# Six single loads become three pair loads of 64 KB pieces, and gamma arrives in four transfers

## The chip, the cores and the metric

The kernel runs on one core of a Trainium2 chip. The metric is the device time of one execution in microseconds (us), lower is better. The kernel before takes about 317.0 us, and equal kernels differ by a few tenths from run to run, so this study is about effects near 0.1%: most of its work went into telling such an effect from noise and into finding where it sits.

## The reference

```python
rms = np.sqrt(np.mean(x ** 2, axis=-1, keepdims=True) + eps)
out = gamma * x / rms
return 0.5 * out * (1 + np.tanh(np.sqrt(2 / np.pi) * (out + 0.044715 * out ** 3)))
```

x has 8 x 1024 rows of 2048 numbers in float32. So 67.1 MB are read and 67.1 MB are written, with an RMS norm over each row and a GELU between.

## The kernel before

The 8192 rows are cut into 16 groups of 512 (4 rows for each of 128 partitions, 4 MB a group). Six buffers ("slots", in three pairs that lie side by side) hold groups in flight. SyncE issues the loads, ScalarE issues the stores. A load waits until the store of the group six places earlier has landed, as it uses the same slot.

```python
def pair_part(a, k):          # two groups: 8 rows = 64 KB in a row for each partition
    n = 2 * R * P
    return a[k * n : (k + 1) * n].rearrange("(p r) d -> p r d", p=P)

def part(a, g):               # one group; 32 KB in a row for each partition
    if g // 2 in (LOAD_PAIR, STORE_PAIR):
        return pair_part(a, g // 2)[:, g % 2 * R : g % 2 * R + R, :]
    return a[g * R * P : (g + 1) * R * P].rearrange("(p r) d -> p r d", p=P)

def load(g):
    nc.sync.dma_start(out=slot[g % SLOTS], in_=part(x2, g))
...
for g in range(G + 1):
    if g < G:
        squares(g, ...)            # ScalarE, the other rows on VectorE
        ...
        inverse_rms(g)             # VectorE and GpSimd
        scale(g, 0, R)             # VectorE: x * gamma
    if g:
        gelu(g - 1)                # ScalarE
        store(g - 1)               # issued by ScalarE
        if g - 1 + SLOTS < G:
            load(g - 1 + SLOTS)    # issued by SyncE
```

Only groups 2 and 3 are loaded as a pair, and only 12 and 13 are stored as one. Each engine works its own list in order, so ScalarE does not start GELU of group g-1 before the squares of group g, for which load g must have landed.

Of the kernel before, what the change touches and what calls it, by code (L numbers as in the profile page):

```python
# [7 lines left out]
FP32 = mybir.dt.float32  # L8
# [3 lines left out]
P = 128  # L12
ROWS = 4
SLOTS = 6

LOAD_PAIR = 1
STORE_PAIR = 6

GW = 128

NARROW = 128

# [1 line left out]
@with_exitstack  # L24
def kernel(
    ctx: ExitStack,
    tc: tile.TileContext,
    x: bass.AP,
    gamma: bass.AP,
    eps: bass.AP,  # L30
    out: bass.AP,
):





    nc = tc.nc
    D = x.shape[-1]
    R = ROWS  # L40
    eps_f = float(eps)
    x2 = x.rearrange("b s d -> (b s) d")
    o2 = out.rearrange("b s d -> (b s) d")
    G = x2.shape[0] // (P * R)

    def pair_part(a, k):

        n = 2 * R * P
        return a[k * n : (k + 1) * n].rearrange("(p r) d -> p r d", p=P)

    def part(a, g):

        if g // 2 in (LOAD_PAIR, STORE_PAIR):
            return pair_part(a, g // 2)[:, g % 2 * R : g % 2 * R + R, :]
        return a[g * R * P : (g + 1) * R * P].rearrange("(p r) d -> p r d", p=P)

    sbuf = ctx.enter_context(tc.tile_pool(name="sbuf", bufs=1))
    psum = ctx.enter_context(
        tc.tile_pool(name="psum", bufs=1, space=bass.MemoryType.PSUM)
    )  # L60
    pair = [
        sbuf.tile([P, 2 * R, D], FP32, name=f"pair{i}") for i in range(SLOTS // 2)
    ]
    slot = [pair[i // 2][:, i % 2 * R : i % 2 * R + R, :] for i in range(SLOTS)]
    spare = sbuf.tile([P, D // GW, GW + 16], FP32, name="spare")
    gamma_row = spare[0:1]
    ones = sbuf.tile([1, P], FP32, name="ones")
    warm = sbuf.tile([1, 1], FP32, name="warm")
    power = sbuf.tile([P, R], FP32, name="power")
    ssq = sbuf.tile([P, G, R], FP32, name="ssq")  # L70
    rstd = sbuf.tile([P, G, R], FP32, name="rstd")
    ms = sbuf.tile([P, R], FP32, name="ms")
    y = sbuf.tile([P, R], FP32, name="y")
    z = sbuf.tile([P, R], FP32, name="z")
    gamma_ps = psum.tile([P, D], FP32, name="gamma_ps")
    junk = psum.tile([P, D], FP32, name="junk")

    def on_vector(g):

        return 1 if g % 3 else 2  # L80

    def load(g):
        nc.sync.dma_start(out=slot[g % SLOTS], in_=part(x2, g))  # L83

    def squares(g, r, n):
        for q in range(r, r + n):
            nc.scalar.activation(  # L87
                out=junk,
                in_=slot[g % SLOTS][:, q, :],
                func=ACT.Square,  # L90
                accum_out=ssq[:, g, q : q + 1],
            )

    def squares_on_vector(g, r, n):
        for q in range(r, r + n):
            row = slot[g % SLOTS][:, q, :].rearrange("p (a b) -> p a b", b=GW)
            nc.vector.scalar_tensor_tensor(  # L97
                out=spare[:, :, 0:GW], in0=row, scalar=1.0, in1=row,
                op0=ALU.bypass, op1=ALU.mult, accum_out=ssq[:, g, q : q + 1],
            )  # L100

    def inverse_rms(g):

        v = nc.vector
        v.tensor_scalar(  # L105
            out=ms, in0=ssq[:, g, :], scalar1=1.0 / D,
            scalar2=eps_f, op0=ALU.mult, op1=ALU.add,
        )
        m_, y_, z_ = ms, y, z
        nc.gpsimd.tensor_tensor(  # L110
            out=y_, in0=m_, in1=power, op=ALU.pow
        )
        v.tensor_tensor(out=z_, in0=m_, in1=y_, op=ALU.mult)  # L113
        v.scalar_tensor_tensor(  # L114
            out=z_, in0=z_, scalar=-0.5, in1=y_, op0=ALU.mult, op1=ALU.mult
        )
        v.scalar_tensor_tensor(  # L117
            out=rstd[:, g, :], in0=z_, scalar=1.5, in1=y_,
            op0=ALU.add, op1=ALU.mult,
        )  # L120

    def scale(g, r, n):
        rows = slot[g % SLOTS][:, r : r + n, :]
        nc.vector.tensor_tensor(  # L124
            out=rows,
            in0=rows,
            in1=gamma_ps.unsqueeze(1).to_broadcast([P, n, D]),
            op=ALU.mult,
        )

    def gelu(g):
        for r in range(R):
            nc.scalar.activation(  # L133
                out=slot[g % SLOTS][:, r, :],
                in_=slot[g % SLOTS][:, r, :],
                func=ACT.Gelu_apprx_tanh,
                scale=rstd[:, g, r : r + 1],
            )

    def store(g):  # L140
        if g:
            if g // 2 != STORE_PAIR:
                nc.scalar.dma_start(out=part(o2, g), in_=slot[g % SLOTS])  # L143
            elif g % 2:
                nc.scalar.dma_start(
                    out=pair_part(o2, g // 2), in_=pair[g // 2 % (SLOTS // 2)]
                )
            return
        src = pair[0].rearrange("p r d -> p (r d)")
        dst = part(o2, 0).rearrange("p r d -> p (r d)")  # L150
        for a, z in ((0, NARROW), (NARROW, R * D)):
            nc.scalar.dma_start(out=dst[:, a:z], in_=src[:, a:z])

    with tc.manual_schedule():
        for g in range(SLOTS):
            if g // 2 != LOAD_PAIR:
                load(g)
            elif g % 2:
                nc.sync.dma_start(
                    out=pair[LOAD_PAIR], in_=pair_part(x2, LOAD_PAIR)  # L160
                )
        nc.scalar.dma_start(
            out=gamma_row[:, :, 0:GW],
            in_=gamma.rearrange("(o a b) -> o a b", o=1, b=GW),
        )
        nc.gpsimd.memset(power, -0.5)  # L166
        nc.vector.memset(warm, 0.0)  # L167
        nc.vector.memset(ones, 1.0)  # L168
        nc.scalar.activation(out=warm, in_=warm, func=ACT.Gelu_apprx_tanh)  # L169
        for k in range(0, D, 512):  # L170
            nc.tensor.matmul(  # L171
                out=gamma_ps[:, k : k + 512],
                lhsT=ones,
                rhs=gamma_row[:, k // GW : (k + 512) // GW, 0:GW],
                start=True,
                stop=True,
            )
        for g in range(G + 1):
            if g < G:
                squares(g, 0, R - on_vector(g))  # L180
                squares_on_vector(g, R - on_vector(g), on_vector(g))
                if g < G - 1:
                    inverse_rms(g)
                    scale(g, 0, R)
                else:
                    scale(g, 0, 1)
                    inverse_rms(g)
                    for r in range(1, R):
                        scale(g, r, 1)
            if g:  # L190
                gelu(g - 1)
                store(g - 1)
                if g - 1 + SLOTS < G:
                    load(g - 1 + SLOTS)
# [35 lines left out]
```

## Time and profile before

| | |
|---|---|
| time | 316.97 us, median of 3 runs; 317.01 with the 3 that were run beside the changed kernel |
| busiest compute engines | ScalarE 66%, VectorE 63% of the span |
| 16 transfer engines | 99% busy, 426 GB/s over the span |
| load queue waits for stores | 236.9 us, 11 times |

A profile like this is read from the transfer row first: no compute engine is near its limit, the transfer engines are. The lines themselves are in the prediction.

### The profile page before, as it was taken

The page shows a single profiled execution, that of the slowest core. Times are in us where ns is not written, and L with a number is a line of the kernel's source. Part 1 is how long each engine was busy: PE and PEld are TensorE (multiplying, and loading weights), DVE is VectorE, ACT ScalarE, POOL GpSimd, SP SyncE. Part 2 cuts the span into 40 slices and gives each one's busy share as a digit, 9 for nine tenths or more (in the row PEclk, how much of TensorE's full clock was granted, in tenths as well). Part 3 has the DMA queues.
Part 4 walks back from the last instruction along what each step waited for, and adds up shares of the span by engine and source line. Part 5 has one row for each costly group of instructions (what it writes and reads, how often), then busy time and mean ns, then how long its engine had stood idle before and what let it go on. Part 6 is the DMA issues. An engine that isn't in the chain of part 4 may idle for free.

```text
span 315.1 us, 457 instructions
## 1 busy us (share of the span) xinstructions
PE 7.2 (2%) x8; PEld 2.5 (1%) x8; DVE 198.5 (63%) x129; ACT 206.9 (66%) x150; POOL 16.4 (5%) x21
## 2 busy tenths in 40 slices
PE   0900000000000000000000000000000000000000
PEld 0300000000000000000000000000000000000000
DVE  0089887988989884639684393668727638781000
ACT  1327869999999749397590965929369295797000
POOL 0010101011010101010010100101001010010000
DMA  8999989999999999999999999999999999999896
GB/s 334 404 462 408 526 339 396 458 402 462 403 463 403 459 408 458 412 453 424 441 424 441 424 441 424 441 428 437 437 428 437 428 437 428 474 399 474 387 445 291
DMA packets 4498, 134.24 MB, mean 426 GB/s; under 512 B 512, under 2 KB 656, under 8 KB 656
## 3 DMA queue, kind: packets, MB, share of 16 engines
q1 hardware_dynamic: 2160, 67.11, 49.7%
q10 hardware_dynamic: 2336, 67.12, 49.3%
q14 instruction: 2, 0.02, 0.0%
HBM read 67.12 MB, written 67.11 MB: 426 GB/s over the span
## 4 chain that ended last, share of the span: by engine, by line
another core or an unknown queue 36%; DMA 36%; ACT 18%; issue 1%; SPq 1%; ACTq 0%
DMA pair<-in_x_dram 21%; DMA out_dram<-pair 15%; ACT pair L133 12%; ACT junk L87 6%; SPq L83 1%; ACTq L143 0%
## 5 line engine op out<-in xcount | busy, mean ns | idle before, releaser
L124 DVE TENSOR_TENSOR pair<-pair,gamma_ps 128x8192 f32<-128x8192 f32 (+1 forms) x19 | 139.2, 7334 | 0.0
L87 ACT ACTIVATE junk<-pair 128x2048 f32<-128x2048 f32 x42 | 79.0, 1881 | 78.7 <-DMA pair<-in_x_dram 76.2
L133 ACT ACTIVATE pair<-pair,rstd 128x2048 f32<-128x2048 f32 x64 | 122.6, 1987 | 2.3 <-DVE pair L124 1.9
L97 DVE SCALAR_TENSOR_TENSOR spare<-pair 128x2048 f32<-128x2048 f32 x22 | 50.4, 2291 | 39.3 <-DMA pair<-in_x_dram 24.6
L110 POOL TENSOR_TENSOR y<-ms,power 128x4 f32<-128x4 f32 x16 | 16.1, 1007 | 260.8 <-DVE ms L105 260.8
L105 DVE TENSOR_SCALAR ms<-ssq 128x4 f32<-128x4 f32 x16 | 2.7, 170 | 26.2 <-ACT junk L87 25.4
L113 DVE TENSOR_TENSOR z<-ms,y 128x4 f32<-128x4 f32 x16 | 2.6, 163 | 19.0 <-POOL y L110 19.0
L87 ACT ACTIVATION_READ_ACCUMULATOR junk<-pair 128x1 f32 x42 | 7.8, 186 | 0.0
L171 PE MATMUL gamma_ps<-spare,ones 1*128 1x512 f32 x8 | 7.2, 1072 | 8.3 <-DMA spare<-in_gamma_dram 8.3
L117 DVE SCALAR_TENSOR_TENSOR rstd<-z,y 128x4 f32<-128x4 f32 x16 | 2.6, 162 | 0.6
L114 DVE SCALAR_TENSOR_TENSOR z<-z,y 128x4 f32<-128x4 f32 x16 | 2.6, 162 | 0.6
L171 PEld LDWEIGHTS gamma_ps<-spare,ones 1*128 1x128 f32 x8 | 2.5, 326 | 11.4 <-issue 11.4
L169 ACT ACT_TABLE_LOAD x1 | 1.3, 1283 | 1.4 <-PEq L211 1.4
L97 DVE DVE_READ_ACCUMULATOR spare<-pair 128x1 f32 x22 | 1.8, 83 | 0.0
L167 DVE MEMSET warm<- 1x1 f32 x1 | 0.1, 59 | 0.8 <-PEq L211 0.8
L169 ACT ACTIVATE warm<-warm 1x1 f32<-1x1 f32 x1 | 0.2, 202 | 0.0
L168 DVE MEMSET ones<- 1x128 f32 x1 | 0.2, 165 | 0.0
L166 POOL MEMSET power<- 128x4 f32 x1 | 0.1, 101 | 0.3 <-POOLq L211 0.3
L211 POOL MEMSET const-float32-0.0<- 128x1 f32 x1 | 0.1, 98 | 0.2 <-issue 0.2
L211 POOL MEMSET const-bfloat16-1.0<- 128x1 bf16 x1 | 0.1, 102 | 0.0
L211 POOL MEMSET const-uint8-127<- 128x1 uint8 x1 | 0.1, 102 | 0.0
L211 POOL MEMSET const-float32-1.0<- 128x1 f32 x1 | 0.1, 98 | 0.0
## 6 DMA issues: line engine op xcount, KB each, us to landing
pair<-in_x_dram SPq DMA_DIRECT2D x14, 4096.0 KB, 25.5
out_dram<-pair ACTq DMA_DIRECT2D x13, 4096.0 KB, 52.4
out_dram<-pair ACTq DMA_DIRECT2D x1, 4032.0 KB, 31.3
out_dram<-pair ACTq DMA_DIRECT2D x1, 64.0 KB, 17.6
spare<-in_gamma_dram ACTq DMA_DIRECT2D x1, 8.0 KB, 7.4
pair<-in_x_dram SPq DMA_DIRECT2D x1, 40.5
out_dram<-pair ACTq DMA_DIRECT2D x1, 30.9
```

What stands on the lines that cost most here:

```text
L83: nc.sync.dma_start(out=slot[g % SLOTS], in_=part(x2, g))
L87: nc.scalar.activation(out=junk, in_=slot[g % SLOTS][:, q, :], func=ACT.Square, accum_out=ssq[:, g, q : q + 1],)
L97: nc.vector.scalar_tensor_tensor(out=spare[:, :, 0:GW], in0=row, scalar=1.0, in1=row, op0=ALU.bypass, op1=ALU.mult, accum_out=ssq[:, g, q ...
L105: v.tensor_scalar(out=ms, in0=ssq[:, g, :], scalar1=1.0 / D, scalar2=eps_f, op0=ALU.mult, op1=ALU.add,)
L110: nc.gpsimd.tensor_tensor(out=y_, in0=m_, in1=power, op=ALU.pow)
L113: v.tensor_tensor(out=z_, in0=m_, in1=y_, op=ALU.mult)
L114: v.scalar_tensor_tensor(out=z_, in0=z_, scalar=-0.5, in1=y_, op0=ALU.mult, op1=ALU.mult)
L117: v.scalar_tensor_tensor(out=rstd[:, g, :], in0=z_, scalar=1.5, in1=y_, op0=ALU.add, op1=ALU.mult,)
L124: nc.vector.tensor_tensor(out=rows, in0=rows, in1=gamma_ps.unsqueeze(1).to_broadcast([P, n, D]), op=ALU.mult,)
L133: nc.scalar.activation(out=slot[g % SLOTS][:, r, :], in_=slot[g % SLOTS][:, r, :], func=ACT.Gelu_apprx_tanh, scale=rstd[:, g, r : r + 1],)
L169: nc.scalar.activation(out=warm, in_=warm, func=ACT.Gelu_apprx_tanh)
L171: nc.tensor.matmul(out=gamma_ps[:, k : k + 512], lhsT=ones, rhs=gamma_row[:, k // GW : (k + 512) // GW, 0:GW], start=True, stop=True,)
```

## The change

The intent: fewer and larger pieces for a kernel that is bound by its transfers. Groups 6 to 11 are loaded in three pairs of 64 KB pieces, each issued when both of its buffers are free. Gamma is cut into four transfers, so that the kernel has 32 transfers in all as before. (Left out of the cut below: the padding of `spare`, which goes from 16 to 4 columns with the narrower rows, and the start, where the six loads are now all made by `load`.)

```diff
-LOAD_PAIR = 1
+LOAD_PAIRS = (1, 3, 4, 5)
-GW = 128
+GW = 32
+CHUNK = 512
...
-        if g // 2 in (LOAD_PAIR, STORE_PAIR):
+        if g // 2 in (*LOAD_PAIRS, STORE_PAIR):
...
     def load(g):
-        nc.sync.dma_start(out=slot[g % SLOTS], in_=part(x2, g))
+        if g // 2 not in LOAD_PAIRS:
+            nc.sync.dma_start(out=slot[g % SLOTS], in_=part(x2, g))
+        elif g % 2:
+            nc.sync.dma_start(
+                out=pair[g // 2 % (SLOTS // 2)], in_=pair_part(x2, g // 2)
+            )
...
-        nc.scalar.dma_start(
-            out=gamma_row[:, :, 0:GW],
-            in_=gamma.rearrange("(o a b) -> o a b", o=1, b=GW),
-        )
+        for k in range(0, D, CHUNK):
+            nc.scalar.dma_start(
+                out=gamma_row[:, k // GW : (k + CHUNK) // GW, 0:GW],
+                in_=gamma[k : k + CHUNK].rearrange("(o a b) -> o a b", o=1, b=GW),
+            )
```

More of the change, by code (lines that the diff above doesn't have):

```diff
@@ L64 @@
     slot = [pair[i // 2][:, i % 2 * R : i % 2 * R + R, :] for i in range(SLOTS)]
-    spare = sbuf.tile([P, D // GW, GW + 16], FP32, name="spare")
+    spare = sbuf.tile([P, D // GW, GW + 4], FP32, name="spare")
     gamma_row = spare[0:1]
@@ L155 @@
         for g in range(SLOTS):
-            if g // 2 != LOAD_PAIR:
-                load(g)
-            elif g % 2:
-                nc.sync.dma_start(
-                    out=pair[LOAD_PAIR], in_=pair_part(x2, LOAD_PAIR)
-                )
-        nc.scalar.dma_start(
-            out=gamma_row[:, :, 0:GW],
-            in_=gamma.rearrange("(o a b) -> o a b", o=1, b=GW),
-        )
+            load(g)
+        for k in range(0, D, CHUNK):
[3 more added lines that the diff above has]
+            )
         nc.gpsimd.memset(power, -0.5)
```

## The prediction

> **What bounds the kernel now.** I read the page from the top: busy shares, the slices, the queues, then the chain that ended last, the waits of the load queue, and the windows. The page first:
>
> ```profile
> span 315.1 us, 457 instructions
> PE 7.2 (2%) x8; PEld 2.5 (1%) x8; DVE 198.5 (63%) x129; ACT 206.9 (66%) x150; POOL 16.4 (5%) x21
> ...
> DMA  8999989999999999999999999999999999999896
> ...
> q1 hardware_dynamic: 2160, 67.11, 49.7%
> q10 hardware_dynamic: 2336, 67.12, 49.3%
> ```
>
> No compute engine is over 66% of the span, while the two queues (q1 has the loads, q10 the stores and gamma) together keep the 16 transfer engines busy 49.7 + 49.3 = 99.0% of it. That is the bound: 0.990 x 315.1 = 312 us of transfer work for each engine, and 3 us of idle at the two ends. The windows of the middle say the same, with a share of 1.00 and about 433 GB/s wherever one looks (last two columns: transfer share, GB/s):
>
> ```profile
> 60.00:120.00 60.00, 0.00 (x0) 0.00 (x0) 51.55 (x34) 51.71 (x39) 4.03 (x4) 1.00 1.01 436
> 120.00:240.00 120.00, 0.00 (x0) 0.00 (x0) 75.65 (x51) 81.32 (x60) 7.05 (x7) 1.00 1.00 433
> ```
>
> The chain shows what looks like a wait that could be removed:
>
> ```profile
> 147.25 0.33 SPq L83
> 147.58 18.99 another core or an unknown queue
> 166.67 0.04 issue
> 166.71 0.33 SPq L83
> 167.03 18.86 another core or an unknown queue
> ```
>
> and so do the waits of the load queue (total us, times, longest):
>
> ```profile
> SPq L83 <- DMA out_dram<-pair: 236.9, 11, 47.3
> ```
>
> Each load of groups 6 to 15 is issued when the store that frees its buffer has landed, one per 19.36 us (127.99 to 244.13 us in the chain is six periods). But one period moves one 4 MB load and one 4 MB store, 8.39 MB in 19.36 us, or 433 GB/s. So the wait of 236.9 us is a queue waiting behind a saturated resource, not the cause of the length. I also added up the single transfer records of the trace: the first data piece starts at 1.74 us, the last ends at 313.93, and the busy time of all pieces divided by 16 is 312.2 us, equal to that interval within 0.1. **There is no hole in the transfers to fill.** What can change the time is the work in them (number and cost of pieces), or a hole that the change opens.
>
> **What the Trainium skill says.** Its page "DMA: Bandwidth & Descriptors", section "Where 436 GB/s comes from", puts the ceiling of the 16 ports at 435 GB/s. The trace's 433 to 436 in the middle windows agrees. The same page, "Queues, rings and completion order", says that each engine takes turns between the queues that have work, a packet at a time. The trace agrees: the 512-byte pieces of the first narrow store start at 36.2, 38.6 and 41.1 us on one engine, one per 64 KB load piece of 2.42 us, and then every 1.23 us beside 32 KB load pieces. The same page, "Anatomy of one DMA", says that transfer engines do not wait on semaphores, the issuing sequencer does. That is how the page shows it: the wait stands in SPq. Its figure of about 2 us for set-up and completion fits too: the store of group 3 has its last piece end at 126.30, and the load that it frees is issued at 127.99, 1.7 us later. Last, "Specifications" warns of pieces under 512 bytes, which gamma's become.
>
> **The change part by part.** The listing of each engine's program shows the same order of instructions on all engines; SP issues 12 transfers for 15, ACT 20 for 17, 32 in all either way. The eight completion semaphores are handed round, so I went through the new waits that this makes.
>
> 1. Bigger pieces. The trace's transfer records give 1,213 ns for a 32 KB piece, 2,418 ns for a 64 KB piece (the pair load of groups 2 and 3 and the pair store of 12 and 13, both the same), 9 ns for a completion write. A pair of single loads costs an engine 16 x 1,213 + 2 x 9 = 19,426 ns; a pair load 8 x 2,418 + 9 = 19,353. Saved: 73 ns a pair, **0.22 us for three pairs**. As the engines are full throughout, all of it lies on the path that sets the end.
>
> 2. Gamma in four. One transfer of sixteen 512-byte pieces (27 ns each, one per engine) and a completion becomes four of sixteen 128-byte pieces. Per engine that is three more pieces and three more completions, at most 3 x (27 + 9) = 0.11 us (an estimate that charges 128 bytes as 512). ACT issues three more transfers at 0.60 us, 1.8 us, before 13.0 us, when it has its first data: hidden. But each small piece takes its turn behind a load piece of 1.21 us, and so does each completion. Before, gamma landed after 7.4 us; four transfers are eight turns, six more than now, so the last may land some 7 us later, about 15 us. The matrix products follow it and may end near 18 us, now 15.4. VectorE's first square waits for them (14.4 us on the page), so group 0 may slip up to 3 us. That costs nothing: ScalarE waits 3.7 us for group 2 at 42.16 anyway, and the six loads alone fill the engines for 6 x 8 x 1.213 = 58 us from 1.7 us on.
>
> 3. Loads of groups 4 and 5 now wait for semaphores of the load of group 0 and the second gamma transfer, both landed by about 15 us, while the loads of groups 1 to 3 are queued until 41.7 us: hidden.
>
> 4. The pair loads wait for two stores. The load of 6 is issued some 13 us later than now, near 83 us for 70. I worked this through in order of time with the durations above, 2 us from issue to first piece, 1.7 us from last piece to the waiter, and turns by piece. (For the kernel before, this walk puts each load and store within about 1 us of the trace, and the last byte at 314.6, where the trace has 313.9.) For the changed kernel:
>    - The load of group 5 ends at 74. From then to 86 the load queue is empty, but stores 1 and 2 (issued at 58 and 70) keep all engines busy, a whole store taking 8 x 1.213 = 9.7 us when alone. Store 1 ends at 81, so the pair 6,7 starts at 86.
>    - Beside 32 KB stores, 64 KB pieces get two thirds of each turn: 8 x (2.418 + 1.213) = 29 us, to 114. Then stores alone again, store 3 ends at 120, pair 8,9 starts at 125, ends at 153. Stores 4 (issued 98) and 5 (127) cover that gap; the gap 153 to 164 has 5 and 6 (142). Pair 10,11 ends at 192, and single loads 12 to 15 follow as now.
>    - A pair takes 39 us from start to start, as two single loads do today: the bytes are the same and so is the rate.
>    ScalarE, whose order puts the squares of group 6 ahead of GELU 5, now waits until 116 us, and store 5 goes out at 127 instead of 108. The store queue still has 5 to 10 us of work at the end of each gap.
>
> Sum: -0.22 + 0.11 at most = -0.1 to -0.2 us; the walk gives -0.19. From 316.97 this makes **316.8 us**.
>
> **Rivals.** *A hole opens.* If the stores run out while a pair load waits for its second buffer, engines idle for up to the 1.7 + 2 us of completion and issue, or longer, as store 5 waits for load 6 and load 6 for store 1. Three such holes would be 3 x 3.7 = 11 us, 328 us. For it speaks that the store queue is fed late, for it depends on a whole pair landing; against it the 5 us or more of stores left in each gap. *Turns by bytes, not pieces.* Then a pair load takes longer, to 124 us, and store 5 goes out at 137; run so, the walk still has no hole and ends at 314.7 instead of 314.4. *Larger pieces gain more* when both directions mix than the pair load alone shows; the pair load's 2,418 ns was measured with no bulk stores beside it. But 32 KB pieces take 1,213 ns with and without mixing, so I expect under 0.5 us. *Gamma holds up the start* by several us: hidden as long as the stores begin before the loads run out near 60 us (part 2). *The end gets worse*: the last stores are issued at 289.4 and the queue has work until 313.9; a shift of 1 us in the last load (the walk has one) is hidden by 20 us of queued stores.
>
> **Range and chances.** Before's three runs span 0.28 us, and my gain is smaller than that. I take 316.8, with 316.2 to 317.3 for 8 in 10: below for a larger gain from 64 KB pieces, above for a small hole or none of the gain. 2% is 6.3 us. Faster by that would need less transfer time than 134 MB at the measured rate allows: 0.005. Slower needs two or three real holes: 0.025. Within: 0.97.
>
> **What would show it.** Right: the share of the two queues still sums to 99%; 65,536-byte load pieces take 2.42 us also beside stores; pair loads last near 29 us where stores run beside them; the chain is still load queue and stores; ScalarE's longest wait for a load grows but its time does not matter; the span falls by 0.1 to 0.3 us. Wrong: digits of 7 or less in the slices between 75 and 165 us, a share below 98%, 64 KB pieces above 2.43 us in the mix, or a wait of ACT's queue to issue a store because of a shared semaphore. If a hole stands at 74 to 86 us, the step about stores covering the gap fails.

## The result, and the profile after

The changed kernel takes 317.32 us (median of 6 runs, 317.30 to 317.73), the kernel before 317.01 (6 runs, 316.78 to 317.64). The ratio is 1.0012 with a 95% interval of 0.9999 to 1.0025. This ratio, like all below, is the mean time of one kernel's fast runs over that of the other's of the same rounds, so it is not quite the ratio of the medians. The predicted 0.2 us of gain became about 0.3 us of loss, and 317.32 is just outside the range. The interval holds 1, so these six runs alone do not tell the loss from noise; the experiments below were made for that.

The page of the changed kernel, with the lines that answer to those of the prediction:

```profile
span 315.7 us, 454 instructions
...
PE 7.9 (2%) x8; PEld 2.1 (1%) x8; DVE 198.0 (63%) x129; ACT 206.9 (66%) x150; POOL 16.4 (5%) x21
...
DMA  8999989999999989999899999999999999999996
...
q1 hardware_dynamic: 1728, 67.11, 49.6%
q10 hardware_dynamic: 2432, 67.12, 49.3%
```

Still 49.6 + 49.3 = 98.9%, and no slice shows a hole. The packets of the load queue fell from 2160 to 1728: 3 pairs x 128 pieces fewer, and 3 x 16 completions fewer. The long windows and those of the three gaps in which only stores run (share of the transfer engines and GB/s at the end of a line; a short window can exceed 1, as a piece is counted whole where it starts):

```profile
60.00:120.00 60.00, 0.00 (x0) 0.00 (x0) 39.85 (x26) 39.37 (x31) 3.02 (x3) 1.00 1.01 435
120.00:240.00 120.00, 0.00 (x0) 0.00 (x0) 83.88 (x54) 91.12 (x67) 7.04 (x7) 1.00 1.00 433
74.00:86.00 12.00, 0.00 (x0) 0.00 (x0) 10.64 (x8) 11.55 (x9) 1.01 (x1) 1.00 1.10 475
114.00:125.00 11.00, 0.00 (x0) 0.00 (x0) 7.94 (x9) 9.30 (x7) 1.01 (x1) 1.00 1.02 441
153.00:164.00 11.00, 0.00 (x0) 0.00 (x0) 4.53 (x7) 9.52 (x8) 1.01 (x1) 1.00 1.02 441
```

The stores fill each gap, as predicted. The new waits are there too, in the chain that ended last (start, us, what), in the stretch around the first pair load:

```profile
55.92 25.43 DMA out_dram<-pair
...
81.56 34.08 DMA pair<-in_x_dram
...
127.30 32.23 DMA out_dram<-pair
```

The chain waits for store 1 until 81.4, then 34 us for pair 6,7, and store 5 is issued at 127.3 us, as the prediction had it (81, 29 us of transfer and latencies, 127). ScalarE's longest wait for a load (last number) grew from 10.1 us in the kernel before, first line, to 19.6 us:

```profile
ACT junk L87 <- DMA pair<-in_x_dram: 76.2, 12, 10.1
...
ACT junk L94 <- DMA pair<-in_x_dram: 73.0, 8, 19.6
```

The waits and the turns came out near the prediction, and still the time went the other way. Two things of this size lie below what the page shows. The trace has start, duration and size of each piece that a transfer engine moved. On one engine the next piece starts 3 to 4 ns before the recorded end of the last, so the records can be strung into 16 chains, one for each engine (in a few traces two chains are swapped somewhere in the middle; the ends are not affected). When each engine finished:

```text
last byte of an engine, us         median of 16   slowest   time of that run   time - slowest
kernel before                         313.24       313.93       316.87             2.94
changed kernel                        313.06       314.54       317.60             3.06
```

The median engine is 0.18 us earlier, which looks like the 0.19 us of the prediction (how much of that is luck is said further down). **The slowest engine is 0.61 us later, and the time goes with the slowest.** And even from there to the end of the run 0.12 us were added.

### The profile page after: what moved, and what is told of

It is laid out like the page before. It is cut to its first block, busy times and chain, and to the rows that moved or that the text cites. A ratio compares the mean times of both kernels' runs of the same rounds, so it can differ in the third digit from the quotient of the medians.

```text
span 315.7 us, 454 instructions
## 1 busy us (share of the span) xinstructions
PE 7.9 (2%) x8; PEld 2.1 (1%) x8; DVE 198.0 (63%) x129; ACT 206.9 (66%) x150; POOL 16.4 (5%) x21
## 3 DMA queue, kind: packets, MB, share of 16 engines
q1 hardware_dynamic: 1728, 67.11, 49.6%
q10 hardware_dynamic: 2432, 67.12, 49.3%
## 4 chain that ended last, share of the span: by engine, by line
DMA 62%; ACT 18%; DVE 8%; issue 2%; POOL 1%; SPq 0%; ACTq 0%; POOLq 0%; DVEq 0%
DMA pair<-in_x_dram 43%; DMA out_dram<-pair 18%; ACT pair L140 12%; ACT junk L94 7%; DVE pair L131 5%; DVE spare L104 2%; POOL y L117 1%; SPq L86 0%; ACTq L150 0%; DVE ms L112 0%; DVE z L120 0%; DVE z L121 0%; DVE rstd L124 0%; SPq L88 0%; POOLq L117 0%
## 5 line engine op out<-in xcount | busy, mean ns | idle before, releaser
L174 PE MATMUL gamma_ps<-spare,ones 1*128 1x512 f32 x8 | 7.9, 1113 | 9.0 <-DMA spare<-in_gamma_dram 9.0
## 6 DMA issues: line engine op xcount, KB each, us to landing
spare<-in_gamma_dram ACTq DMA_DIRECT2D x4, 2.0 KB, 10.1
```

The source lines that it names most:

```text
L174: nc.tensor.matmul(out=gamma_ps[:, k : k + 512], lhsT=ones, rhs=gamma_row[:, k // GW : (k + 512) // GW, 0:GW], start=True, stop=True,)
```

## The experiments

**Noise, and which part of the change costs.** Four kernels: both kernels again, the pairs without the gamma split, the gamma split without the pairs.

```diff
 # pairs_only: the changed kernel, with
+GW = 128
+CHUNK = 2048
 # gamma4_only: the changed kernel, with
+LOAD_PAIRS = (1,)
```

> The kernel before, unchanged, against itself: shows how far a ratio of equal kernels strays. All theories: ratio within 0.05% of 1 (0.15 us). If it strays by 0.1% (0.3 us) the measured difference of the change is not told from noise.

> The changed kernel again. Noise theory: ratio between 0.9993 and 1.0005, since mean work per transfer engine falls by 0.1 us. Theory of a real cost: ratio again 1.0010 or more (+0.3 us). In the trace either way: mean end of the 16 engines 0.1 us or less from that of before, slowest engine later by stretched pieces, at other places than in the first trace.

> The pair loads without the gamma split. If the pairs carry a cost (restart of the load queue after a gap, 64 KB pieces that stretch): ratio 1.0010 or more. If gamma carries it: ratio 0.9993 (-0.2 us). Noise theory: 0.9993 too, with an interval that holds 1.

> Gamma in four, loads as before. If gamma carries the cost: ratio 1.0010 or more (+0.3 us). If the pairs carry it, or noise: ratio 1.000 to 1.0003 (at most +0.1 us), with the matrix products ending some 2 us later and nothing after 42 us changed.

Measured, beside the kernel before at 317.18 us on the same chip: the kernel before again 1.0002 (0.9989 to 1.0016), the changed one 1.0011 (0.9999 to 1.0024), pairs alone 1.0011 (0.9997 to 1.0025), gamma alone 1.0000 (0.9988 to 1.0013). Each interval by itself holds 1, but 1.0012, 1.0011 and 1.0011 for three sets of kernels with the pairs, against 1.0002 and 1.0000 for two without, point to about 0.35 us that comes with the pairs. Gamma in four shows no cost, though in the changed kernel its last transfer landed at 14.3 us and VectorE waited 16.0 us for the matrix products instead of 14.4: hidden, as predicted.

**Gap, piece size, or placing in memory.** The first set: the gap without the larger piece, smaller pieces without a gap, more pairs, and work for one engine alone.

```diff
 # late_singles: the kernel before, groups 6 to 11
+                    if n % 2:
+                        load(n)        # the odd one first: it waits for the later store
+                        load(n - 1)
 # half_pieces: the kernel before, loads and stores of groups 6 to 11
+            return a[g * R * P : (g + 1) * R * P].rearrange("(h p r) d -> p h (r d)", h=2, p=P)
 # one_engine: the kernel before, after the first five loads
+        nc.sync.dma_start(out=extra, in_=x2[0:17, 0:1024])
 # more_pairs: pairs_only, with
+LOAD_PAIRS = (1, 3, 4, 5, 6, 7)
```

> The kernel before, with the loads of 7 and 6 (9 and 8, 11 and 10) issued odd one first, at the place where the pair was issued: the gap of the load queue of the changed kernel, but in 32 KB pieces. Restart theory (the first load pieces after a gap of the load queue are stretched on a few of the 16 transfer engines, and the slowest engine sets the end): ratio 1.0010 to 1.0020, as the pairs' -0.2 us is missing; stretched load pieces near 87 and 165 us. Piece theory (64 KB pieces beside stores are what stretches): ratio 1.000 to 1.0005.

> The kernel before, loads and stores of groups 6 to 11 in 16 KB pieces. Work theory (8 ns for each piece more, all of it on the path): 6 x 8 x 2 = 96 pieces more for an engine, +0.77 us, ratio 1.0024; a 16 KB piece takes about 610 ns. If pieces cost nothing on the path: 1.000.

> The kernel before, with one load more that is never used: 17 rows of 4 KB, all of which one transfer engine has to move, some 17 x 0.16 = 2.7 us of its time (an estimate from 32 KB in 1.213 us). Slowest-engine theory: the end moves by 1.9 to 2.7 us (ratio 1.006 to 1.0085), as that engine ends up to 0.8 us ahead of the slowest without it. Mean-work theory: 2.7 / 16 = 0.17 us, ratio 1.0005.

> Pair loads also for 12 to 15, gamma in one: five gaps of the load queue instead of three. Restart theory: ratio 1.0010 to 1.0025, the slowest engine 1 us or more behind the median one. Work theory alone: 5 x 0.073 = 0.37 us less, ratio 0.9988. If the gaps near the end let the stores run dry: a hole in the transfers and some us more.

All four came out slower than expected, and they taught the most. Against 316.96 us: late singles 1.0105 (320.33 us), half pieces 1.0090 (320.25), one engine 1.0547 (334.43), more pairs 1.0348 (328.00).

*More pairs* opened the hole that the prediction had as its first rival. Windows around it, share of the transfer engines next to last:

```profile
262.00:274.00 12.00, 0.00 (x0) 0.00 (x0) 2.30 (x2) 3.23 (x3) 0.00 (x0) 1.00 0.99 429
274.00:285.00 11.00, 0.00 (x0) 0.00 (x0) 6.91 (x5) 10.55 (x9) 1.01 (x1) 1.00 0.01 6
285.00:297.00 12.00, 0.00 (x0) 0.00 (x0) 10.71 (x11) 11.50 (x9) 1.01 (x1) 1.00 1.01 437
```

For 11 us almost no byte moves. The pair of groups 14 and 15 lands at 269 us at once, where load 14 alone had landed at 249. ScalarE's squares of 14 stand ahead of GELU 13, so the pair store of 12 and 13 is issued at 284.4 us instead of 264.0, and the store queue had run dry at 274. The change under study ends its pairs at group 11 and has no such hole.

*One engine* has the same kind of hole, 18 us long:

```profile
274.00:292.00 18.00, 0.00 (x0) 0.00 (x0) 11.33 (x8) 13.62 (x11) 1.01 (x1) 1.00 0.04 18
```

The 17 extra pieces took 159 ns each, 2.7 us in sum, as estimated, and 0.17 us as a mean over the engines. But each took a turn of the load queue: the 17 turns lasted from 75.7 to 104.2 us, with 14 store pieces between them that took 1.2 to 2.3 us each (why most took more than the usual 1.21 is open). So the loads of this engine fell behind. In the trace its last load piece ends at 287.2 us, those of the others by 268, 19 us earlier. ScalarE waited for load 14 until 277.9 us, in the kernel before until 250.3: one late engine holds up a whole load. **With turns by piece, a small piece cost its queue a turn, whatever its size.** The expectation had counted bytes.

*Late singles* put the gap and 32 KB pieces together. A pair of single loads beside 32 KB stores gets half the turns by time, not two thirds, and needs 39 us after a gap of 12. So the loads run late: most engines end their last load at 271 us instead of 267, one at 276. No hole opened, but load pieces were stretched (they took up to 1.0 us longer than their usual 1,213 ns) on 15 engines at about 95 us and on most at about 177. The sum of such stretches after 55 us is 19.9 us over the 16 engines, 1.2 us for each, and by 1.2 us the median engine ended later (314.5 for 313.2); the slowest one ended at 317.2. So the larger piece seems to be more than fewer pieces: it gives the load queue longer turns, which make up for the gap. The split pair below tests that.

*Half pieces*: a 16 KB piece takes 611 ns, so a cut adds 2 x 611 - 1,213 = 9 ns of recorded durations. As records overlap by 3 to 4 ns, that is some 5.5 ns of time, and 0.5 us for 96 cuts (an estimate). The median engine ended 0.6 us later; six engines ended 2.4 to 3.6 us after the median one, and the time rose by 3.3 us. That the cost of a cut is on the path is thus in keeping with the run, not shown by it. In this trace too pieces were stretched, loads by 9.4 us in sum over the engines and most of them at 148 to 153 us, stores by 9.1 us, although the load queue has no gap. Why is open.

The second set tells the gap from the placing in memory, which the prediction had overlooked: a pair deals 8 neighbouring rows to a partition, so the stores of groups 6 to 11 also go out in 32 KB pieces 64 KB apart.

```diff
 # pitch_only: the kernel before, with
+        if g // 2 in (LOAD_PAIR, 3, 4, 5, STORE_PAIR):
 # split_pair: pairs_only, each pair of 6 to 11 as two transfers
+            both = ((0, 8),) if g < SLOTS else ((0, 5), (5, 8))
 # start_pair: pairs_only, with
+LOAD_PAIRS = (1, 2)
```

> The kernel before with single loads, issued as before, but rows dealt to partitions as in the changed kernel: loads and stores of groups 6 to 11 in 32 KB pieces that lie 64 KB apart in memory instead of 32. No gap in the load queue, no larger piece. If the placing in memory is what costs (part of the change that the prediction overlooked): ratio 1.0010. If gaps or piece size cost: 1.0000, with no stretched load piece at 87 or 165 us but those behind an instruction fetch.

> The pairs of 6 to 11 with gamma in one, each pair as two transfers one right after the other, of 40 KB and 24 KB pieces, both waiting for both stores. Gap, order of rows and placing as in the changed kernel; the largest piece is gone, and the engine has 8 pieces and a completion more for each pair. Restart theory: as pairs_only plus 0.2 us, ratio 1.0010 to 1.0025, stretched load pieces near 87 and 165 us. Piece-size theory: ratio 1.0000 to 1.0005. If the ratio is near 1.01, as with late_singles, shorter turns of the loads after a gap are what costs, and the 64 KB piece is what keeps the cost of the gap small.

> Pair loads for groups 2, 3 and 4, 5 only, gamma in one: a 64 KB piece more at the start, where nothing is waited for, no gap. Work theory: 0.07 us less, ratio 0.9998. Piece-size theory: ratio 1.0003 or more, with stretched 64 KB pieces between 49 and 74 us.

Against 317.11 us: placing alone 0.9995 (0.9982 to 1.0008), so it shows no cost. A second pair at the start, without a gap, 1.0004 (0.9992 to 1.0016), median 317.28. The pair as 40 KB and 24 KB pieces 1.0057 (1.0031 to 1.0083). There the loads again had shorter turns, ended 7 us or more late, and a small hole opened. The trace is of a run of 320.44 us, one of the two slowest; the other four took 317.97 to 318.96, and whether they have the hole is not on record. The first line is the kernel before, the others are the split pair:

```profile
274.00:279.00 5.00, 0.00 (x0) 0.00 (x0) 3.75 (x8) 5.00 (x3) 1.01 (x1) 1.00 0.98 426
...
262.00:274.00 12.00, 0.00 (x0) 0.00 (x0) 5.00 (x7) 9.99 (x9) 1.01 (x1) 1.00 1.00 431
274.00:279.00 5.00, 0.00 (x0) 0.00 (x0) 5.00 (x1) 4.23 (x3) 0.00 (x0) 1.00 0.60 256
```

The ratio lies between the 1.0025 at most of one theory and the 1.01 of another, so it decides less than hoped. But it agrees with the reading of the late singles: with a gap in the load queue, it is the 64 KB piece that keeps the loads in time (with it the last load piece ended at 269 to 270 us in three traces, here at 278.0).

**Do stretched pieces follow the gap?** In all three traces with the three pairs so far, load pieces were stretched on single engines soon after a gap, above all at 86.7 to 87.2 us and at 164.6 to 165.0 us, right behind the starts of pair loads at 85.5 and 163.7. Two more kernels have one gap, early or late, and two runs are one more trace each of the changed kernel and of the kernel before.

```diff
 # gap_first / gap_last: pairs_only, with
+LOAD_PAIRS = (1, 3)
+LOAD_PAIRS = (1, 5)
```

> Pair load for 6, 7 alone, gamma in one: one gap of the load queue, about 74 to 86 us. Restart theory: load pieces stretched by over 0.1 us between 84 and 100 us beyond the one or two behind an instruction fetch (302 ns of fetch, then 241 or 531 ns of stretch), and none between 160 and 185 us. Ratio 1.0000 to 1.0012. If stretches come at 165 us too, they are not the gap's.

> Pair load for 10, 11 alone: one gap, about 152 to 168 us. Restart theory: stretched load pieces between 165 and 185 us on a few engines, none but those of a fetch before. Ratio 1.0000 to 1.0012. If they come near 87 us and not here, they are not the gap's.

> One more trace of the changed kernel. Restart theory: stretch of load pieces after 55 us, summed over the 16 engines, 1.2 to 4.1 us as in the three traces with pairs so far, the slowest engine ending 0.9 us or more after the median one, the median one at 313.1 us.

> One more trace of the kernel before. Restart theory: stretch of load pieces after 55 us 0.8 to 1.4 us in sum (the two behind instruction fetches are 0.77), as in four of the five traces without gaps so far; the fifth had an event on all engines at 203 us. Median engine ending at 313.2 us, slowest at 313.9.

```text
stretch of load pieces after 55 us, sum over the 16 engines, us (each line one kernel, each number one trace)
no gap:      before 0.8, 8.8, 0.8;  gamma alone 1.3;  placing 0.8;  start pair 1.0;  before + 2 activations 0.8
three gaps:  changed 3.2, 4.1, 5.3;  changed + 1 activation 7.3;  pairs alone 1.2;  pairs + 1 activation 4.1
one gap:     early 1.1;  late 0.8
```

(The kernels with extra activations come below.) In every trace of these seven without a gap, 0.77 to 0.78 us of the sum are two single pieces that follow a fetch of instructions: the trace has such a fetch as a record of 8,192 bytes on a queue of its own, it keeps one transfer engine from its pieces for 302 ns, and the load piece behind it mostly takes 241 to 571 ns more. The 8.8 is one trace with an event on all 16 engines at 203 us; that run took 317.98 us. With three gaps five traces of six have 3 us or more. But pairs alone has 1.2, less than the 1.3 of gamma alone, which has no gap. And the third trace of the changed kernel was expected at 1.2 to 4.1 and has 5.3. With one gap there is little: beyond what follows a fetch, pieces of 0.13 and 0.04 us in the early one, and none in the late one, where 165 to 185 us was expected. So the expectation for the late gap failed. The two kernels still were slower than expected, 317.47 and 317.65 us against 317.08 (1.0016 with 1.0000 to 1.0033, and 1.0017 with 1.0002 to 1.0032). So stretches are more with three gaps in most traces, but that a gap by itself makes them is not shown, and the half pieces have them with no gap.

How far the slowest engine ended after the median one, in the same traces:

```text
slowest engine's last byte less the median one's, us (each number one trace)
no gap:      before 0.7, 1.1, 0.7;  gamma alone 1.2;  placing 0.7;  start pair 0.7;  before + 2 activations 0.9
three gaps:  changed 1.5, 1.2, 1.5;  changed + 1 activation 1.4;  pairs alone 1.0;  pairs + 1 activation 1.1
one gap:     early 1.0;  late 1.0
```

The lag is larger with gaps on average, but the two kinds overlap, and gamma alone has 1.2 though its ratio is 1.0000: one trace of a kernel does not prove a cost. As far as the chains can be strung, in all seven traces without a gap the slowest engine is one that served a fetch of instructions, at 94 to 109 us. With three gaps it is mostly another one, with stretched load pieces; but in pairs alone and in both kernels with one gap the slowest engine has no stretched piece after 55 us at all. So the stretches explain a part of the traces, not the loss as such.

**What lies outside the span.** For each timed run both the time and the traced span are known, the span to 0.1 us. Their difference turned out to be the steadiest number: 1.78 us in 47 runs of the kernel before, never outside 1.73 to 1.83. In the changed kernel it is 1.98 as a mean, though with more scatter, 1.80 to 2.07 and once 2.41. Listed for all kernels, it goes not with the loads but with the number of ScalarE's instructions in the trace (its 150 compute instructions on the page, and its waits and issues):

```text
ScalarE instructions   rest by 4   time - span, us (mean)
185                        1       before 1.78, placing 1.81, split pair 1.78
189                        1       gamma alone 1.78
186                        2       early gap 1.82, half pieces 1.85, one engine 1.84
183                        3       late gap 2.10
184                        0       pairs alone 1.93, start pair 1.94, more pairs 1.90, late singles 1.94
188                        0       changed 1.98 and 2.00
```

Three kernels change that number and nothing else, by repeating a one-element activation at the start:

```diff
         nc.scalar.activation(out=warm, in_=warm, func=ACT.Gelu_apprx_tanh)
+        nc.scalar.activation(out=warm, in_=warm, func=ACT.Gelu_apprx_tanh)
```

> The changed kernel with one tiny activation more at the start, which does nothing for the result. Over twelve kernels the time outside the traced span (time of a run less span of the same run) goes with the number of ScalarE's instructions in the trace: 185, 186 and 189 give 1.78 to 1.84 us, 184 and 188 give 1.90 to 2.00, 183 gives 2.10: by the rest on division by 4. The changed kernel has 188, this one should have 189. If the rest matters: 1.78 us outside the span, 0.2 us faster than the changed kernel, ratio to the kernel before 1.0005. If it is the pairs themselves that lengthen it: again 2.0 us, ratio 1.0011.

> The kernel before with two tiny activations more at the start: 187 ScalarE instructions for 185. If the rest on division by 4 matters: 2.10 us outside the span, ratio 1.0010, with no change to loads at all. If not: 1.78 us, ratio 1.0000.

> Pairs with gamma in one, and one tiny activation more: 185 ScalarE instructions for 184. If the rest matters: 1.78 us outside the span, 0.15 us faster than without, ratio 1.0006; what is then left is the pairs' own cost inside the span, 0.1 to 0.25 us. If not: 1.93 us, ratio 1.0011.

The page of the kernel before with two more (457 instructions and x150 without them):

```profile
span 315.3 us, 459 instructions
...
PE 7.2 (2%) x8; PEld 2.5 (1%) x8; DVE 198.5 (63%) x129; ACT 207.3 (66%) x152; POOL 16.4 (5%) x21
```

and the page of the changed kernel with one more:

```profile
span 315.8 us, 455 instructions
...
PE 7.9 (2%) x8; PEld 2.1 (1%) x8; DVE 198.0 (63%) x129; ACT 207.1 (66%) x151; POOL 16.4 (5%) x21
```

Outside the span: 2.03 us for the kernel before with 187 instructions (each of 5 runs between 1.99 and 2.09), 1.76 for the changed kernel with 189, 1.77 for pairs alone with 185. **So the 0.2 us more that the changed kernel has outside the span go with the count of ScalarE's instructions**, which three more issues for gamma and another number of waits raised from 185 to 188, and not with any transfer. Times: the kernel before with 187 instructions 317.33 us for 317.03, 1.0009 (0.9997 to 1.0022): a loss like that of the change, with no load touched, though this interval too holds 1.

The other two had been expected at 1.0005 and 1.0006 and came out at 1.0012 and 1.0012 (317.37 and 317.53 us). Their 0.2 us outside was gone, but inside the span they lost more than expected: mean span 0.38 and 0.48 us above that of the kernel before on that chip, where the changed kernel and pairs alone had 0.16 and 0.20 on theirs. So taking the 0.2 us away made neither kernel faster, and that this term is a loss of its own, and not time that moved from inside the span to outside, rests on the one kernel with 187 instructions. Kernels without a gap of the load queue (the kernel before again, gamma alone, placing, start pair, two activations) had +0.10, +0.04, -0.18, -0.02, +0.04 inside the span; the two with one gap had +0.42 (early) and +0.25 (late), as much as those with three. So the cost of the pair loads inside the span is 0.2 to 0.5 us, with a scatter of 0.1 to 0.2 from runs and chips, and it is not shown to grow with their number.

No version beat the kernel before by more than noise: placing alone at 0.9995 has an interval that holds 1.

## Why the prediction was wrong

- **The bound was right.** The transfers were full before and after (99.0% and 98.9%), and there was no hole in the gaps.
- **The usual durations were right.** 64 KB load pieces took 2,418 ns also beside stores (median of the 384 in the three new pairs), completions 9 ns, 128-byte gamma pieces 13 ns (512-byte ones took 27). Gamma landed at 14.3 us, as predicted near 15. But a sign of being wrong that the prediction had named came true: 11 of the 384 pieces took more than 2.43 us, the longest 3.20.
- **The schedule was right to half a microsecond, in part by luck.** Pair loads ran from 85.5 to 114.1, 124.8 to 152.8 and 163.7 to 191.9 us, predicted 86 to 114, 125 to 153 and 164 to 192. Turns by piece held. But the first pair load was issued at 81.6 us, not near 83, and from issue to first piece the three took 3.9 to 4.0 us, where the prediction had 2: the two errors nearly cancel.
- **The work term was too large.** It added up recorded durations: 3 x 73 ns less for the pairs and 52 ns more for gamma are -0.17 us, as in the traces. But records of one engine overlap by 3 to 4 ns, and an engine has 21 records fewer, so only some 0.09 us of time are saved (an estimate from these numbers). That the median engine ended 0.18 us earlier is then partly luck; gamma alone, which saves nothing, has it at 313.08 us too. And even the sum of the recorded durations did not fall: for each engine it is 312.2 us in two traces of the kernel before (the third had the event at 203 us) and 312.2 to 312.3 in three of the changed one, where the stretches after 55 us (of loads and stores) took 0.25 to 0.37 us instead of 0.08. The same overlap, about 1.0 us for an engine, is in the 312.2 us from which the prediction concluded that there is no hole; the chains show that there is none all the same.
- **The step that failed** is in the prediction's part 1: "As the engines are full throughout, all of it lies on the path that sets the end." The path is not the mean of 16 full engines but the slowest of them. In all twenty traces, from 316.86 to 334.54 us, the time of the traced run was that engine's last byte plus 2.94 to 3.44 us. The slowest ended 0.7, 1.1 and 0.7 us after the median one in three traces of the kernel before, and 1.5, 1.2 and 1.5 us in three of the changed one. In place of -0.19 us, the kernels with three pairs measured +0.16 to +0.48 us inside the span. Why their slowest engine is later stays open.
- **A term was missing**: 0.2 us outside the span, which go with ScalarE's instruction count. The prediction took the time as span plus a constant. The mean of what is added is 1.78 for 185 instructions and 1.98 for 188.
- In the six runs of the result the two are about equal: the means differ by 0.37 us (the medians by 0.31), of which 0.20 lie outside the span, if the kernel before has its 1.78 us there as in its other runs, and the other 0.17 inside, where -0.19 had been predicted. The range, 316.2 to 317.3, had allowed a small hole or no gain, but no loss in an engine's lag.
- **The rivals.** A hole did not open here; it does with two pairs more (11 us) and with pairs in 40 and 24 KB pieces (part of 5 us). Turns by bytes is refuted by the 28 to 29 us that a pair load took. Gamma was hidden. The placing in memory was not named; it shows no cost.
- **What stays open**: why the slowest engine ends later with pair loads, why a load piece is stretched by 0.1 to 1.0 us, why this befalls few engines, and whether one gap suffices (the traces of the kernels with one gap do not show it, though their spans rose); also why the count of ScalarE's instructions matters by its rest on division by 4.

## What to carry to other kernels

When all 16 transfer engines are full, ask for the last of them: a saving of 0.1 to 0.2 us in the work of each reaches the end only if nothing holds one engine up, and the page's share of 99% does not show that. When adding up recorded durations, look first whether the records overlap. Where two queues share an engine piece by piece, the size of a piece is also the length of a turn: larger load pieces win time against the stores, and here 17 tiny pieces on one engine put its loads 19 us behind. For effects near 0.1%, compare span and time of each run and check the instruction counts before giving a reason, and run the unchanged kernel against itself.

## What the Trainium skill lacked or had wrong

- "DMA: Bandwidth & Descriptors", section "Queues, rings and completion order": it gives turns by packet, and the trace agrees, with one piece a turn. It lacks what follows for authors: 17 pieces of 159 ns put one engine's loads 19 us behind and the kernel 17 us (1.0547).
- The same page, "Rules for kernel authors", "Many small transfers": it advises large transfers for their overhead. The rule speaks of whole transfers, not of the pieces within one, and no page weighs the length of a turn. Here, in transfers of 4 to 8 MB, a cut added 8 to 9 ns of recorded durations (2 x 1,213 - 2,418; 2 x 611 - 1,213), and the length of the turn seems to matter more: the ratio for pairs after a gap was 1.0011 in 64 KB pieces and 1.0057 in 40 and 24 KB pieces.
- "Perfetto Trace Analysis", section "What 'DMA-bound' means": it says that the bound may be specific engines of the 16. The runs agree, and give a size: the slowest ended 0.7 to 3.6 us after the median one in kernels without a hole.
- "Runtime: NRT & Kernel Launch", section "Instruction fetch mechanics": it calls the cost of fetching the next block mostly hidden, with blocks of 16 KiB. The trace has fetches as single records of 8,192 bytes, each of which keeps a transfer engine from its pieces for 302 ns and is mostly followed by a load piece 241 to 571 ns longer than usual. In all seven traces without a gap the engine that ended last had served one, so for a kernel bound by its transfers that is not hidden.
- No page has it that the time outside the traced span changes with the number of ScalarE's instructions: 1.76 to 1.81 us for 185 and 189, 1.82 to 1.85 for 186, 1.9 to 2.1 for 183, 184, 187 and 188 (means of a kernel's runs).
